# First MLP product of a hybrid encoder layer: Strassen's seven half-size products, with blocks of x1 kept in SBUF and in DRAM

## The chip, the cores and the metric

The kernel runs on one core of a Trainium2 chip. The metric is the device time of one execution in microseconds (us), lower is better.

## What is computed

The reference is one layer of a streaming encoder for 1024 tokens of width 1024 in float32: a LayerNorm, a mixer (stick-breaking attention, a Conformer convolution and a short gated convolution, joined by an output projection), a second LayerNorm whose result is called x1 here, and an MLP with a residual and a last LayerNorm:

```python
h = layer_norm(DEEPNORM_ALPHA * h + mix, ln_mix_g[l], ln_mix_b[l])          # x1, 1024 x 1024
ff = jnp.square(jax.nn.relu(h @ w_ff1[l])) @ w_ff2[l]                       # 1024 -> 4096 -> 1024
h = layer_norm(DEEPNORM_ALPHA * h + ff, ln_ff_g[l], ln_ff_b[l])
```

Only the MLP and the way into it bear on this change.

## The kernel before

Every large product is done in float32r, with each operand split in two: `split` (L126) has ScalarE cast the source to a high part h (L127) and VectorE subtract h from the source to get a low part l (L128). A product is then the three matmuls h·h, h·l and l·h, added up in PSUM.

The mixer ends with eight token tiles of 128 rows, handled in the order 6, 7, 4, 5, 0, 1, 2, 3 (`mix_tile`, `mix_tiles`, L726 to L757). Each tile gets its matmuls with `w_out` (L629), its sums (L733), its LayerNorm statistics on ScalarE and GpSimd (L737 to L748, L90 to L92) and its two rows of LayerNorm on VectorE (L121, L123); after that it is a tile of x1 in `acc`. `x1_columns` transposes a tile on TensorE (L169) and splits it into `x1h` and `x1l`, which hold all of x1 with the model width on the partitions.

The MLP runs over eight groups of 512 hidden units (`ff_group`, L904). A group has two products.

- The first one, x1 with the group's columns of `w_ff1`, is plain. `load_cols` loads 128 columns of the weights and splits them; `ff1_chunk` (L794) does 24 matmuls of 128x512 for half of the tokens into one PSUM bank (L800), then ScalarE takes the ReLU (L804) and VectorE squares it (L805). Four units of 128 columns and two halves of the tokens make 8 x 24 = 192 matmuls. The result lies in `ra[0]` and `ra[1]`.
- The second one, with the group's 512 rows of `w_ff2`, already goes by Strassen's scheme in Winograd's form. The hidden units and the tokens, and the units and the output columns, are cut in two halves each; seven products of half the size stand for eight. `a_part` and `b_part` split the operands of each into a ring of five buffers; GpSimd and VectorE form the sums and differences (`gsum`, L819; `early_sums`, L920). Each product is 4 x 6 = 24 matmuls into four banks (`product`, L847). The banks are added to one or more quarters of `acc` between the products (`add_to`, L857 to L861): four of the seven products go on accumulating in the same banks, so that each intermediate state can be read.

PSUM has four banks with the tag `g` for these products, three with `t` for transposes and one with `o`. An order of the instructions on each engine is made when the program is built, by a planner with its own estimates: it takes what the program lists first among what it thinks ready. Each engine and each DMA queue then works strictly in that order; SyncE (SP) issues nearly all loads.

For the first group, work starts before all of x1 is there: the chunks for the token half of tiles 4 to 7 go first (L979 to L995). In the last group `finish_rows` (L876) does the last LayerNorm, for tokens 0 to 511 with GpSimd's help and for the others on VectorE alone.

Of the kernel before, what the change touches and what calls it, by code (L numbers as in the profile page):

```python
# [15 lines left out]
P = 128  # L16
D = 1024
# [24 lines left out]
def hybrid_layer(ctx: ExitStack, tc, x, meta_tokens, ln_in_g, ln_in_b, w_in, w_conf_dw, b_conf_dw,  # L42
# [40 lines left out]
    yscr = dr.tile([4, P, S], F32, name="yscr")  # L83

# [674 lines left out]
    def x1_columns(i):  # L759
        transpose_split(acc[:, order[i], :], P, x1h, x1l, order[i] * P)  # L760

# [13 lines left out]
    x1h = x1p.tile([P, KT, S], F32R, name="x1h")  # L775
    x1l = x1p.tile([P, KT, S], F32R, name="x1l")
    done = 0
    for i in range(FIRST, 8):
        run(mix_tiles(i, i + 1))
        while done < i - 1 and done < 2 * (i - FIRST + 1):  # L780
            x1_columns(done)
            done += 1
    x = acc[:, order[7], :]
    ln_rows_dve(x, x, P, lnq[order[7]], *norm)
# [7 lines left out]
    ra = {}  # L792

    def ff1_chunk(j, w, c):  # L794

        pg = ps_g([P, 512])
        i = 0
        for k in range(KT):
            for a, b in ((0, x1h), (0, x1l), (1, x1h)):
                nc.tensor.matmul(pg, lhsT=w[a][:, k, :], rhs=b[:, k, c * 512:(c + 1) * 512],  # L800
                                 start=(i == 0), stop=(i == 3 * KT - 1))
                i += 1
        sq = cst.tile([P, 512], F32, tag="sq", bufs=1, name="sq")
        nc.scalar.activation(out=sq, in_=pg, func=AF.Relu)  # L804
        nc.vector.tensor_tensor(out=ra[j // 2][:, j % 2, HALF[c]], in0=sq, in1=sq, op=ALU.mult)  # L805

    def ff1_open(g, j):
        if j % 2 == 0:
            ra[j // 2] = wA.tile([P, 2, S], F32, tag="ff", bufs=2, name="relu2")
        u = 4 * g + (j + 2) % 4  # L810
        return halves(load_cols(w_ff1, u * P))

    def ff1(g, j):
        w = ff1_open(g, j)
        for c in range(2):
            ff1_chunk(j, w, c)
# [3 lines left out]

    def ring(name):
        return ffp.tile([P, 2, 2, 512], F32R, tag="ring", bufs=5, name=name)

    def a_part(src):
        hl = ring("a_hl")
        split(hl[:, 0], hl[:, 1], src)
        return hl

    def b_part(src):
        hl = ring("b_hl")  # L830
        split(hl[:, 0], hl[:, 1], src)
        return hl

    def w2_load(g):

        rb = [ffp.tile([P, 2, D], F32, tag=f"w2_{h}", bufs=1, name=f"w2_{h}") for h in range(2)]
        for h in (1, 0):
            r0 = (4 * g + 2 * (1 - h)) * P
            nc.sync.dma_start(out=rb[h], in_=w_ff2[r0:r0 + 2 * P, :].rearrange("(u p) c -> p u c", p=P))
        return rb  # L840
# [9 lines left out]

    def add_to(th, n, banks, first, sums=None, tts=range(4)):
        for tt in tts:
            t = 4 * th + tt
# [9 lines left out]
    def ln_ff_rows():  # L863

        rows, banks = [], []
        for tag, row in (("t1", ln_ff_g), ("s1", ln_ff_b)):
            r = ffp.tile([P, D], F32, tag=tag, bufs=1, name="ln_ff")
            bcast_row(r, row[0], nc.sync)
            rows.append(r)
        for i in range(4):  # L870
            bk = ps_t([P, 512]) if i < 3 else ps_o([P, 512])
            nc.scalar.activation(out=bk, in_=rows[i // 2][:, HALF[i % 2]], func=AF.Copy, scale=ROOT_D if i < 2 else 1.0)
            banks.append(bk)
        return rows[1], banks[:2], banks[2:]

    def finish_rows(t, sm, fb, gps, bps):  # L876
# [5 lines left out]
        junk = raw_tile("junk")  # L882
        nc.scalar.activation(out=junk, in_=a, func=AF.Square, bias=mean, accum_out=sm[:, 2:3])
        y = f32(big(name="y")[:, 0])
# [6 lines left out]
        if t < 4:  # L891
# [4 lines left out]
        for n in range(2):  # L896
            nc.vector.scalar_tensor_tensor(out=a[:, HALF[n]], in0=y[:, HALF[n]], scalar=rs[:, 0:1], in1=bps[n],
                                           op0=ALU.mult, op1=ALU.add)
            if t == NT - 1:
                (nc.sync, nc.scalar)[n].dma_start(out=os_[rows, HALF[n]], in_=a[:, HALF[n]])  # L900
        if t < NT - 1:
            nc.sync.dma_start(out=os_[rows, :], in_=a)

    def ff_group(g, opened=()):  # L904
# [5 lines left out]
        t1 = ffp.tile([P, 2, 512], F32, tag="t1", bufs=1, name="t1")  # L910
        gsum(t1, b12, b11, ALU.subtract)
        gsum(b12, b22, b12, ALU.subtract)
        for j in (2, 3, 0):
            if j not in opened:
                ff1(g, j)
        a11, a21 = (ra[0][:, :, h] for h in HALF)
        a12, a22 = (ra[1][:, :, h] for h in HALF)
        s1 = ffp.tile([P, 2, 512], F32, tag="s1", bufs=1, name="s1")

        def early_sums(u, eng):  # L920
            eng.tensor_tensor(out=s1[:, u], in0=a21[:, u], in1=a22[:, u], op=ALU.add)
            eng.tensor_tensor(out=a21[:, u], in0=a11[:, u], in1=a21[:, u], op=ALU.subtract)

        early_sums(0, nc.gpsimd)
        w = ff1_open(g, 1)
        ff1_chunk(1, w, 0)
        b, a = b_part(b21), a_part(a12)
        b_, a_ = b_part(b11), a_part(a11)
        gsum(b11, b22, t1, ALU.subtract)
        gsum(b21, b21, b11, ALU.subtract)  # L930
        gsum(a11[:, 0], s1[:, 0], a11[:, 0], ALU.subtract)
        ff1_chunk(1, w, 1)
        early_sums(1, nc.vector)
# [92 lines left out]
```

## Time and profile before

| | us |
|---|---|
| median of 3 runs | 1265.03 (1262.49 to 1266.19) |
| the profiled execution | 1265.27 |
| its span, first to last instruction | 1263.5 |

The profile is of one execution. It gives the busy time of each engine (PE is TensorE, PEld its weight loads, DVE VectorE, ACT ScalarE, POOL GpSimd, SP SyncE) and the chain of waits that ended last. A stretch's table tells what each engine did in that time, and the granted clock of TensorE as a share of 2.4 GHz. A matmul's own duration includes its way through the pipeline, so that its price in a dense row is the time from start to start.

### The profile page before, as it was taken

What the parts mean: (1) busy time and instruction counts of PE and PEld (TensorE: products, weight loads), DVE (VectorE), ACT (ScalarE), POOL (GpSimd) and SP (SyncE); (2) the same over time, 40 slices, a digit from 0 to 9 for tenths busy, and PEclk for the clock granted to TensorE, in tenths of its full rate; (3) what the DMA queues carried; (4) which work ended last, traced back from release to release, by engine and by line L of the source; (5) the groups of instructions that cost most, each with busy time, mean ns of one, the idle gap of its engine ahead of it and who ended that gap; (6) DMA issues with size and microseconds to landing.
All of it is one profiled execution on the core that took longest, in us unless ns stands there. A gap on an engine that the chain in (4) does not pass through costs nothing.

```text
span 1263.5 us, 15743 instructions
## 1 busy us (share of the span) xinstructions
PE 1186.0 (94%) x6126; PEld 1023.2 (81%) x6126; DVE 923.3 (73%) x1236; ACT 478.9 (38%) x883; POOL 235.3 (19%) x275
## 2 busy tenths in 40 slices
PE   5999996899989798998999999999999999999993
PEld 5999996789888687886888888888888888888882
DVE  6799976978788699777494684846947559467388
ACT  5522115656566445444332222313323123232244
POOL 2300002010000100144221312213212131121215
PEclk9999997989999899998999999999999999999997
DMA  9313111021011611203121111111211212012013
GB/s 291 121 39 86 59 51 51 17 51 34 17 34 51 200 34 67 84 16 102 34 67 34 50 67 34 52 65 35 82 30 38 67 50 84 18 51 67 1 34 133
DMA packets 71466, 78.97 MB, mean 63 GB/s; under 512 B 2345, under 2 KB 57936, under 8 KB 71392
## 3 DMA queue, kind: packets, MB, share of 16 engines
q1 hardware_dynamic: 67168, 67.97, 17.1%
q0 software_dynamic: 2304, 4.20, 1.7%
q10 hardware_dynamic: 1920, 5.81, 1.3%
q8 instruction: 48, 0.79, 0.3%
q14 instruction: 26, 0.21, 0.1%
HBM read 63.28 MB, written 10.49 MB: 58 GB/s over the span
## 4 chain that ended last, share of the span: by engine, by line
PE 67%; DVE 9%; ACT 3%; issue 2%; POOL 1%; DMA 1%; DVEq 0%; ACTq 0%; SPq 0%
PE ps_g L800 28%; PE ps_g L847 22%; PE ps_g L209 6%; PE ps_g L629 5%; DVE keepp L462 2%; PE ps_t L512 2%; PE ps_g L454 2%; PE ps_o L485 1%; PE ps_o L488 1%; DVE beta L464 1%; ACT keepp L458 1%; DVE acc L861 1%; DVE al L128 1%; DMA q_hl<-q_hl 1%; DVE a_hl L128 1%
## 5 line engine op out<-in xcount | busy, mean ns | idle before, releaser
L847 PE MATMUL ps_g<-b_hl,a_hl 128*128 128x512 f32 x1344 | 306.2, 389 | 2.3 <-DVE a_hl L128 2.3
L800 PE MATMUL ps_g<-x1h,w_hl 128*128 128x512 f32 x992 | 307.3, 389 | 0.0
L847 PEld LDWEIGHTS ps_g<-b_hl,a_hl 128*128 128x128 f32 x1344 | 252.2, 188 | 55.1 <-DVE a_hl L128 2.7
L209 PE MATMUL ps_g<-xh,w_hl 128*128 128x346 f32 (+4 forms) x1024 | 260.8, 334 | 0.9 <-ACT beta L459 0.9
L800 PEld LDWEIGHTS ps_g<-x1h,w_hl 128*128 128x128 f32 x992 | 186.2, 188 | 38.5
L800 PE MATMUL ps_g<-x1l,w_hl 128*128 128x512 f32 x496 | 193.0, 389 | 0.0
L805 DVE TENSOR_TENSOR relu<-sq 128x512 f32<-128x512 f32 x64 | 56.2, 878 | 185.9 <-ACT sq L804 185.9
L209 PEld LDWEIGHTS ps_g<-xh,w_hl 128*128 128x128 f32 x1024 | 181.4, 193 | 10.0 <-ACT beta L459 1.1
L209 PE MATMUL ps_g<-xl,w_hl 128*128 128x346 f32 (+4 forms) x512 | 171.0, 334 | 0.7 <-DVE xl L128 0.7
L804 ACT ACTIVATE sq<-ps_g 128x512 f32<-128x512 f32 x64 | 38.3, 598 | 285.4 <-PE ps_g L800 284.7
L859 DVE TENSOR_TENSOR acc<-ps_g,acc 128x512 f32<-128x512 f32 x192 | 126.5, 681 | 14.5 <-PE ps_g L847 13.5
L800 PEld LDWEIGHTS ps_g<-x1l,w_hl 128*128 128x128 f32 x496 | 93.1, 188 | 19.4
L209 PEld LDWEIGHTS ps_g<-xl,w_hl 128*128 128x128 f32 x512 | 99.0, 193 | 5.0 <-DVE xl L128 1.0
L128 DVE TENSOR_TENSOR w_hl<-raw,w_hl 128x1024 fp32r<-128x1024 f32 x59 | 93.2, 1580 | 11.8 <-ACT w_hl L127 11.6
L127 ACT CAST a_hl<-relu 128x1024 fp32r<-128x1024 f32 x48 | 50.5, 1053 | 123.6 <-PE ps_g L847 78.2
L462 DVE TENSOR_TENSOR_SCAN keepp<-keepp 128x912 f32<-128x912 f32 (+7 forms) x64 | 87.7, 1380 | 11.4 <-ACT keepp L458 10.9
L128 DVE TENSOR_TENSOR a_hl<-relu,a_hl 128x1024 fp32r<-128x1024 f32 x48 | 70.6, 1470 | 24.1 <-ACT a_hl L127 23.8
L127 ACT CAST w_hl<-raw 128x1024 fp32r<-128x1024 f32 x59 | 61.8, 1047 | 61.5 <-PE ps_g L209 31.7
L284 DVE SCALAR_TENSOR_TENSOR cacc<-glu,prm,cacc 128x482 f32<-128x482 f32 (+3 forms) x120 | 82.7, 743 | 0.3
L128 DVE TENSOR_TENSOR b_hl<-w,b_hl 128x1024 fp32r<-128x1024 f32 x48 | 67.1, 1398 | 0.5 <-ACT b_hl L127 0.2
L629 PE MATMUL ps_g<-w_hl,y 128*128 128x512 f32 x240 | 65.2, 409 | 1.8 <-DVE w_hl L128 1.7
L454 PE MATMUL ps_g<-ks,q_hl 128*128 128x456 f32 (+8 forms) x224 | 58.6, 364 | 8.4 <-ACT beta L459 3.9
(194 smaller groups left out, 1556.1 us busy)
## 6 DMA issues: line engine op xcount, KB each, us to landing
raw<-in_w_ff_dram SPq DMA_DIRECT2D x32, 512.0 KB, 4.1
w<-in_w_ff_dram SPq DMA_DIRECT2D x16, 1024.0 KB, 5.0
raw<-in_w_in_dram SPq DMA_DIRECT2D x22, 512.0 KB, 4.2
xt<-in_x_dram SPq DMA_DIRECT2D x8, 512.0 KB, 5.8
h_scr<-ht ACTq DMA_DIRECT2D x8, 512.0 KB, 3.2
q_hl<-q_hl POOLq DMA_DIRECT2D x16, 256.0 KB, 3.1
raw<-in_w_out_dram SPq DMA_DIRECT2D x8, 512.0 KB, 3.6
acc<-h_scr SPq DMA_DIRECT2D x8, 512.0 KB, 7.3
```

The lines of the kernel that those rows point to most:

```text
L127: nc.scalar.copy(out=h, in_=src)
L128: nc.vector.tensor_tensor(out=l, in0=src, in1=f32(h), op=ALU.subtract)
L209: nc.tensor.matmul(dst[:, :cw], lhsT=w[:, a, k, :], rhs=b[:, k, c0:c0 + cw], start=(i == 0), stop=(i == 3 * KT - 1))
L284: nc.vector.scalar_tensor_tensor(out=acc, in0=glu[j][:, o + k:o + k + n], scalar=prm[:, j, k:k + 1], in1=acc, op0=ALU.mult, op1=ALU.add)
L454: nc.tensor.matmul(zp[:, :cm], lhsT=qs[h][:, m, i * P:(i + 1) * P], rhs=ks[:, h, c0:c0 + cm], start=(m == 0), stop=(m == 1 and not last))
L462: nc.vector.tensor_tensor_scan(out=rev, data0=rev, data1=rev, initial=1.0, op0=ALU.mult, op1=ALU.bypass)
L629: nc.tensor.matmul(dst, lhsT=y[a][:, t * P:(t + 1) * P], rhs=w[b][:, n * 512:(n + 1) * 512], start=(i == 0), stop=(i == last))
L800: nc.tensor.matmul(pg, lhsT=w[a][:, k, :], rhs=b[:, k, c * 512:(c + 1) * 512], start=(i == 0), stop=(i == 3 * KT - 1))
L804: nc.scalar.activation(out=sq, in_=pg, func=AF.Relu)
L805: nc.vector.tensor_tensor(out=ra[j // 2][:, j % 2, HALF[c]], in0=sq, in1=sq, op=ALU.mult)
L847: nc.tensor.matmul(banks[tt], lhsT=a[:, x, u, tt * P:(tt + 1) * P], rhs=b[:, y, u, :], start=(start and i == 0), stop=(i == 5), skip_group ...
L859: nc.vector.tensor_tensor(out=a, in0=banks[tt], in1=a, op=ALU.add)
```

## The change

The first product goes by the same seven products. The group's 1024 x 512 weights are cut in halves both ways (a11, a12, a21, a22, each 512 x 256), x1 in halves of tokens and of width. Of x1's seven blocks and block combinations, each split in high and low, three stay in SBUF (`xt1`, `xt2`, `xt3`); the others share two tiles, X and Y, and come from the DRAM tensor `xscr` in each group, 2 MB each. Only the first group finds the first two in place. `x1_first` transposes and splits the plain blocks of the last four token tiles; `x1_second` forms differences of the token halves on GpSimd, and transposes and splits them and another plain block, of which two go to DRAM by way of `stage`.

A product is two banks of 12 matmuls (`product1`). Between products the banks are copied by ScalarE (`keep_sum`) or added to such a copy, and squared after a ReLU, by VectorE (`relu2`, `relu2_bank`). The weights of a group are loaded in two DMAs of 1 MB; GpSimd forms the weight sums s1, a21, a11 and a12 in place. In the second product the order of the seven products is another, the sums of the hidden values go to VectorE (`vsum`), the ring has four buffers in place of five, and which half of the tokens counts as the first is swapped (`tok`).

The core of the diff (loads, names and the last LayerNorm's buffers left out; what is not shown of the second product is its unchanged chain):

```diff
+    xscr = dr.tile([4, P, 2, 4, 512], F32, name="xscr")
...
-    def x1_columns(i):
-        transpose_split(acc[:, order[i], :], P, x1h, x1l, order[i] * P)
...
+    xb21, xb11, xt1, xt3 = [x_tile(x1p, tag) for tag in ("X", "Y", "T1", "T3")]
+
+    def x1_block(hl, src, cols):
+        pt = ps_t([P, 4, P])
+        for k in range(4):
+            nc.tensor.transpose(out=pt[:, k], in_=src[:, k * P:(k + 1) * P], identity=ident)
+        split(hl[:, 0, :, cols], hl[:, 1, :, cols], pt)
...
+    for i, x in enumerate((xb21, xb11)):
+        nc.sync.dma_start(out=xscr[i], in_=f32(x))
...
+    def product1(a, x, banks, start):
+        for j in range(2):
+            i = 0
+            for k in range(4):
+                for u, v in ((0, 0), (0, 1), (1, 0)):
+                    nc.tensor.matmul(banks[j], lhsT=a[:, u, k, j * P:(j + 1) * P], rhs=x[:, v, k, :],
+                                     start=(start and i == 0), stop=(i == 11), skip_group_check=True)
+                    i += 1
...
+    def keep_sum(r, th, bk):
+        for j in range(2):
+            nc.scalar.copy(out=r[:, j, HALF[th]], in_=bk[j])
+
+    def relu2(r, th, bk):
+        for j in range(2):
+            a = r[:, j, HALF[th]]
+            nc.vector.tensor_tensor(out=a, in0=bk[j], in1=a, op=ALU.add)
+            nc.vector.scalar_tensor_tensor(out=a, in0=a, scalar=0.0, in1=a, op0=ALU.max, op1=ALU.mult)
...
+    def x1_second(i, dt, stage):
+        t = order[i]
+        cols = slice(t * P, (t + 1) * P)
+        x, y = acc[:, t], acc[:, 4 + t]
+        d1, d2, d3, d4 = (dt[:, n // 2, HALF[n % 2]] for n in range(4))
+        gsum(d1, x[:, HALF[0]], y[:, HALF[0]], ALU.subtract)
+        gsum(d2, x[:, HALF[1]], d1, ALU.subtract)
+        gsum(d3, x[:, HALF[1]], x[:, HALF[0]], ALU.subtract)
+        gsum(d4, y[:, HALF[1]], d2, ALU.subtract)
+        x1_block(xt2, d2, cols)
+        x1_block(xt1, d1, cols)
+        c = slice(t % 2 * P, t % 2 * P + P)
+        x1_block(stage[0], x[:, HALF[1]], c)
+        x1_block(xt3, d3, cols)
+        x1_block(stage[1], d4, c)
+
+    def first_product(g, start=None):
...
+        s1 = raw_tile("s1").rearrange("p (k c) -> p k c", k=4)
+        gsum(s1, a21, a22, ALU.add)
+        gsum(a21, a11, a21, ALU.subtract)
...
+        if first:
+            pc, aa = start
+        else:
+            x = load_x("X", 0)
+            a = part(a12, 4)
+            pc = banks(2)
+            product1(a, x, pc, True)
+            aa = part(a11, 4)
+        keep_sum(r0, 0, pc)
+        x = xb11 if first else load_x("Y", 1)
+        pa = banks(2)
+        product1(aa, x, pa, True)
+        relu2(r0, 0, pa)
+        gsum(a11, s1, a11, ALU.subtract)
+        a = part(a11, 4)
+        if first:
+            second_half()
+        product1(a, xt2, pa, False)
+        keep_sum(r1, 0, pa)
+        gsum(a12, a12, a11, ALU.subtract)
+        a = part(s1, 4)
+        product1(a, xt1, pa, False)
+        keep_sum(r1, 1, pa)
+        x = load_x("X", 2)
+        a = part(a12, 4)
+        product1(a, x, pa, False)
+        relu2_bank(r0, 1, pa)
+        a = part(a21, 4)
+        pb = banks(2)
+        product1(a, xt3, pb, True)
+        relu2(r1, 1, pb)
+        x = load_x("Y", 3)
+        a = part(a22, 4)
+        product1(a, x, pb, False)
+        relu2(r1, 0, pb)
+        return r0, r1
...
+        b, a = part(b11, 2), part(a11, 2)
+        gsum(b11, b12, b11, ALU.subtract)
+        vsum(s1, a21, a22, ALU.add)
+        vsum(a21, a11, a21, ALU.subtract)
+        vsum(a11, s1, a11, ALU.subtract)
+        pa = banks(4)
+        product(a, b, pa, True)
+        add_to(0, 0, pa, first)
...
+    def second_half():
+        for n in range(2):
+            stage = [ring("stage").rearrange("p s (k c) -> p s k c", k=4) for _ in range(2)]
+            for i in (4 + 2 * n, 5 + 2 * n):
+                x1_second(i, ffp.tile([P, 2, D], F32, tag=f"w2_{i % 2}", bufs=1, name="diffs"), stage)
+            for j in range(2):
+                nc.sync.dma_start(out=xscr[2 + j][:, :, :, 256 * n:256 * n + 256], in_=f32(stage[j]))
```

## Rows read from the trace of the kernel before

**Rows 1.** The page's first part: busy us, share of the span, instructions.

```profile
PE 1186.0 (94%) x6126; PEld 1023.2 (81%) x6126; DVE 923.3 (73%) x1236; ACT 478.9 (38%) x883; POOL 235.3 (19%) x275
```

**Rows 2.** Stretches: length, busy us of each engine, granted clock, DMA share, GB/s.

```profile
601.38:634.35 32.97, 32.97 (x145) 27.29 (x146) 14.62 (x15) 10.25 (x13) 8.34 (x5) 1.00 0.12 32
...
754.03:797.55 43.52, 43.52 (x194) 36.04 (x193) 18.04 (x15) 10.99 (x14) 10.16 (x5) 1.00 0.13 37
797.55:835.63 38.08, 38.08 (x170) 31.53 (x169) 34.43 (x42) 11.66 (x12) 7.77 (x4) 1.00 0.21 69
...
1205.55:1263.50 57.95, 38.38 (x169) 31.11 (x167) 50.45 (x89) 25.40 (x34) 19.04 (x22) 0.88 0.24 91
```

**Rows 3.** The chain of waits in order of time, one group: start, us, engine, line.

```profile
754.03 43.52 PE ps_g L800 x192
797.55 38.08 PE ps_g L847 x168
```

**Rows 4.** VectorE in order of time, a second product: start us, us, instruction.

```profile
800.16 1.22 DVE L128 TENSOR_TENSOR w_hl<-raw,w_hl 128x1024 fp32r<-128x1024 f32 x1
801.29 0.68 DVE L859 TENSOR_TENSOR acc<-ps_g,acc 128x512 f32<-128x512 f32 x1
801.89 0.68 DVE L922 TENSOR_TENSOR relu<-relu 128x512 f32<-128x512 f32 x1
802.49 0.68 DVE L859 TENSOR_TENSOR acc<-ps_g,acc 128x512 f32<-128x512 f32 x1
...
816.82 1.21 DVE L128 TENSOR_TENSOR b_hl<-w,b_hl 128x1024 fp32r<-128x1024 f32 x1
```

**Rows 5.** VectorE in order of time, where GpSimd works beside it.

```profile
778.14 3.41 DVE L128 TENSOR_TENSOR w_hl<-raw,w_hl 128x1024 fp32r<-128x1024 f32 x1
...
805.00 2.42 DVE L128 TENSOR_TENSOR a_hl<-relu,a_hl 128x1024 fp32r<-128x1024 f32 x1
...
823.31 1.28 DVE L859 TENSOR_TENSOR acc<-ps_g,acc 128x512 f32<-128x512 f32 x2
```

**Rows 6.** GpSimd in order of time, the same group and one sum of the last.

```profile
777.75 2.73 POOL L819 TENSOR_TENSOR w<-w,w 128x1024 f32<-128x1024 f32 x1
...
795.96 2.14 POOL L819 TENSOR_TENSOR relu<-s,relu 128x512 f32<-128x512 f32 x1 [4.33 <-DVE a_hl L128]
803.92 2.42 POOL L819 TENSOR_TENSOR relu<-relu,relu 128x1024 f32<-128x1024 f32 x1 [5.82 <-DVE relu L934]
823.27 2.41 POOL L819 TENSOR_TENSOR t<-w 128x1024 f32<-128x1024 f32 x1 [16.93 <-DMA w<-in_w_ff_dram]
...
1196.11 1.29 POOL L921 TENSOR_TENSOR s<-relu,relu 128x512 f32<-128x512 f32 x1 [7.64 <-DVE relu L805]
```

**Rows 7.** ScalarE in order of time, the first casts of two operand pairs.

```profile
813.99 1.05 ACT L127 CAST a_hl<-relu 128x1024 fp32r<-128x1024 f32 x1 [3.51 <-PE ps_g L847]
...
819.35 1.05 ACT L127 CAST a_hl<-relu 128x1024 fp32r<-128x1024 f32 x1 [3.36 <-PE ps_g L847]
```

**Rows 8.** DMA issues: transfer, queue, count, KB each, median us to landing.

```profile
w<-in_w_ff_dram SPq DMA_DIRECT2D x16, 1024.0 KB, 5.0
```

**Rows 9.** Stretches of 5 us on the way into the MLP, columns as above.

```profile
580.00:585.00 5.00, 3.17 (x13) 2.57 (x14) 5.00 (x7) 2.77 (x7) 1.70 (x5) 0.50 0.50 127
585.00:590.00 5.00, 5.00 (x20) 4.21 (x20) 3.93 (x6) 1.68 (x3) 0.00 (x0) 0.70 1.06 384
```

**Rows 10.** TensorE in order of time on the way into the MLP.

```profile
574.09 0.40 PE L629 MATMUL ps_g<-wo,y_low 128*128 128x512 f32 x1
576.99 1.73 PE L169 MATMUL ps_t<-ident,acc 128*128 128x128 f32 x8 [2.50 <-DVE x1l L128]
...
584.71 0.80 PE L800 MATMUL ps_g<-x1h,w_slot 128*128 128x512 f32 x1
```

**Rows 11.** VectorE in order of time, the last token tile's second LayerNorm row.

```profile
585.77 1.27 DVE L123 SCALAR_TENSOR_TENSOR acc<-acc,rs,norm 128x1024 f32<-128x1024 f32 x1
```

**Rows 12.** SyncE's queue in order of time: the first weights of the MLP.

```profile
565.44 17.21 SPq L139 DMA_DIRECT2D raw<-in_w_ff_dram  x3
```

More of the change, by code (lines that the diff above doesn't have):

```diff
@@ L779, in hybrid_layer @@
         run(mix_tiles(i, i + 1))
-        while done < i - 1 and done < 2 * (i - FIRST + 1):
-            x1_columns(done)
+        while done < 4 and done < 2 * (i - FIRST + 1):
+            x1_first(done)
             done += 1
@@ L784, in hybrid_layer @@
     ln_rows_dve(x, x, P, lnq[order[7]], *norm)
-    NG = NF // 4
-    HALF = slice(0, 512), slice(512, 1024)
[L792 to L816, printed above, removed]
+    for i, x in enumerate((xb21, xb11)):
+        nc.sync.dma_start(out=xscr[i], in_=f32(x))
+    attw.release()
+    x1q = pool("x1q", side="right")
+    xt2 = x_tile(x1q, "T2")
@@ new lines, in w1_block, with w1_load @@
+    def w1_block(k, c0):
+        raw = raw_tile("w1_raw").rearrange("p (k c) -> p k c", k=4)
+        nc.sync.dma_start(out=raw, in_=w_ff1[512 * k:512 * k + 512, c0:c0 + 256].rearrange("(k p) c -> p k c", p=P))
+        return raw
+    def w1_load(g):
+        rk = []
+        for k in (1, 0):
+            raw = wA.tile([P, 4, 512], F32, tag="w", bufs=2, name="w1_raw")
+            nc.sync.dma_start(out=raw, in_=w_ff1[512 * k:512 * k + 512, 512 * g:512 * g + 512].rearrange("(k p) c -> p k c", p=P))
+            rk.append(raw)
+        return rk[1], rk[0]
@@ L818, in gsum, with w1_view, vsum, part @@
+    def w1_view(hl):
+        return hl.rearrange("p s (k c) -> p s k c", k=4)
     def gsum(dst, a, b, op):
         nc.gpsimd.tensor_tensor(out=dst, in0=a, in1=b, op=op)
+    def vsum(dst, a, b, op):
+        nc.vector.tensor_tensor(out=dst, in0=a, in1=b, op=op)
     def ring(name):
-        return ffp.tile([P, 2, 2, 512], F32R, tag="ring", bufs=5, name=name)
-    def a_part(src):
-        hl = ring("a_hl")
+        return ffp.tile([P, 2, D], F32R, tag="ring", bufs=4, name=name)
+    def part(src, k):
+        hl = ring("hl").rearrange("p s (k c) -> p s k c", k=k)
@@ L863, in ln_ff_rows @@
     def ln_ff_rows():
-        rows, banks = [], []
-        for tag, row in (("t1", ln_ff_g), ("s1", ln_ff_b)):
-            r = ffp.tile([P, D], F32, tag=tag, bufs=1, name="ln_ff")
+        rows, bks = [], []
+        for row in (ln_ff_g, ln_ff_b):
+            r = raw_tile("ln_ff")
             bcast_row(r, row[0], nc.sync)
@@ L909, in ff_group @@
         b21, b22 = (rb[1][:, :, h] for h in HALF)
-        t1 = ffp.tile([P, 2, 512], F32, tag="t1", bufs=1, name="t1")
+        t1 = raw_tile("t1").rearrange("p (u c) -> p u c", u=2)
         gsum(t1, b12, b11, ALU.subtract)
[L912 to L918, printed above, removed]
@@ L932, in ff_group @@
-        ff1_chunk(1, w, 1)
-        early_sums(1, nc.vector)
-        nc.vector.tensor_tensor(out=a11[:, 1], in0=s1[:, 1], in1=a11[:, 1], op=ALU.subtract)
-        def banks():
-            return [ps_g([P, 512]) for _ in range(4)]
-        pc = banks()
-        product(a, b, pc, True)
-        add_to(0, 0, pc, first)
-        pa = banks()
-        product(a_, b_, pa, True)
-        add_to(0, 0, pa, False, sums)
-        b, a = b_part(b11), a_part(a11)
-        gsum(a12, a12, a11, ALU.subtract)
+        gsum(b12, b22, t1, ALU.subtract)
@@ L958, in ff_group @@
-        pb = banks()
+        b, a = part(b21, 2), part(a12, 2)
+        gsum(b21, b21, b12, ALU.subtract)
+        pc = banks(4)
+        product(a, b, pc, True)
+        add_to(0, 0, pc, False, sums)
+        b, a = part(b11, 2), part(a21, 2)
+        pb = banks(4)
         if not last:
@@ L965, in ff_group @@
             return
-        b_, a_ = b_part(b21), a_part(a22)
-        for t in range(4):
-            finish_rows(t, sums[t], *ln)
+        b_, a_ = part(b21, 2), part(a22, 2)
+        for tt in range(4):
+            finish_rows(tok(0, tt), sums[tok(0, tt)], *ln, True, False)
         for step in (0, 1, 4, 2, 5, 3, 6, 7):
             tt = step % 4
+            t = tok(1, tt)
             if step < 4:
```

123 lines of the change are left out of this document (67 added, 56 removed).

## The prediction

> **What bounds the kernel now.** I read the busy times first: TensorE 1186.0 us of a span of 1263.5, VectorE 923.3 [rows 1]. A share over the whole span says little, so the next view is the table of stretches, for the stage that the change touches [rows 2]. From 601.38 us to 1205.55 us TensorE is busy in every microsecond of every stretch, at full clock. A group of the MLP takes 81.60 us: 43.52 for the first product and 38.08 for the second. The chain of waits says the same in its own way: for a whole group it names nothing but matmuls, x192 in 43.52 us, then x168 in 38.08 us [rows 3]. Both give 0.2267 us for a matmul of 128x512 (43.52/192 and 38.08/168), so here time is the number of matmuls. VectorE is the next engine: 18.04 us of the first stretch, but 34.43 us of the 38.08 of the second [rows 2]. That second number is where I expect the trouble.
>
> **What the change removes.** A unit of the first product takes 2x24 matmuls, a group of four 192. Seven products of 24 are 168, which is what the second product already has. So each group loses 24 x 0.2267 = 5.44 us of matmuls; eight groups lose 43.5 us. If TensorE stayed as dense, a group would take 76.16 us.
>
> **What it adds to VectorE and GpSimd in groups 1 to 7.** Durations from start to start: a split's subtraction of 1024 columns 1.13 us, an addition of a PSUM bank 0.60, a half-size sum 0.60 [rows 4]. The evictions of the first product become six pairs of bank addition and multiplication (0.6 each, the latter taken as a half sum) and two multiplications alone, in place of eight: 8.4 for 4.8. Splits go from 18 to 21 (+3.4). Sums on VectorE go from three of 512 to four of 1024 (+2.7). So some 53 us undisturbed, where the same count gives 44 before (measured 18.04+34.43 = 52.47 [rows 2]; the rest is time in which GpSimd held it up). GpSimd has eight sums of about 2.4 us, 19 us, near its 10.16+7.77 = 17.93 before. ScalarE has three more casts (1.05) and two instructions of 0.6 in place of two: +3 on 10.99+11.66 = 22.65 us, far from a bound.
>
> The disturbance is visible: a split of 1.13 us took 3.41 us at 778.14, beside a sum of GpSimd from 777.75 to 780.48, and 2.42 us at 805.00 beside one from 803.92; the two bank additions at 823.31, beside GpSimd's sum from 823.27, took 1.28 together, as ever [rows 5, 6]. A split that meets a sum loses some 1.3 us (2.42-1.13), up to 2.3; below I take 1.25.
>
> Now the second product's 38.08 us of matmuls. Before: 11 splits (12.4), 28 additions (16.8), three half sums and one multiplication (2.4) make 31.6, and 2.8 of holding up gives the measured 34.43. After: 13 splits (14.7), 28 additions (16.8), two full sums (2.3) and the tail of the last eviction (1.2) make 35. GpSimd's sums in this stretch go from three to four or five (the next group's weights are now summed here): at 1.25 each 5 to 6 us. Together 40 to 41 us, which is 2 to 3 us over. The overrun may run on into the next first product, where VectorE has some 24 of 38 us to do (8 splits 9.0, evictions 7.2, two sums 2.3, held up 5). TensorE feels it only when an operand pair is late. A pair's casts start when the product two before it lets go of its buffers, and take two casts and two splits: from 813.99 on ScalarE to 818.0 on VectorE (816.82+1.21); the next pair's casts, released by TensorE in the same way, began at 819.35, so 1.3 us were spare [rows 4, 7]. The ring of five buffers becomes one of four, which leaves that pattern. I put half of the overrun on TensorE, 1.2 us a group; the bounds are 0 and 3.
>
> **Bank handovers in the first product.** Before, a bank was reused three chunks later, 16 us. Now four products add onto banks that an engine must read between two products: 2.72 us (12 x 0.2267) from the end of a bank's product to its next use. ScalarE's copy (some 0.6, twice) fits; VectorE's addition (some 0.7, twice) fits unless it finds VectorE in a held-up split. Included in the 1.2 above; priced alone as a rival.
>
> **Reloads.** Four blocks of 2 MB a group come back: 8 MB on top of the 4 MB of weights. 12 MB in 76 us is 158 GB/s; 1 MB landed in 5.0 us, and a stretch moved 384 GB/s at a full DMA share [rows 8, 9]. Block X is asked for a second time when its first product is over, and needed three products later, 16.3 us; 2 MB take 6 to 10 us. Behind it on SyncE's queue wait block Y (four products of slack) and the group's w2 (five), which need 6 MB in some 33 us, 182 GB/s. Covered, so nothing; without the cover a late block would cost its lateness, up to 4 us.
>
> **Group 0 and the way in.** The last matmul of the mix starts at 574.09, and the last token tile's LN ends at 587.0 (585.77+1.27) [rows 10, 11]. Before, 48 matmuls were done between transposes by 601.38 and the other 144 ran to 634.35 [rows 2]. After, products one and two need only the first four tiles (48 matmuls, done by about 594). Product three needs the differences of all tiles: 14 of 16 GpSimd sums of 512 columns at 1.29 (2.14 if VectorE holds them up, [rows 6]), and three sums of weights at 2.4, 25 to 37 us from about 580, then a transpose and split, 2 us: 607 to 619, I take 610. Its 80 transposes, at 1.73 for eight at the low clock [rows 10], are 17 us at most, and its 20 bank splits 12 on VectorE: both lie beside GpSimd's chain. TensorE idles some 10 us; the granted clock stood at 0.50, the 1.2 GHz level, after waits like the 2.5 us before 576.99, and a matmul took 0.80 us instead of 0.40 [rows 9, 10]: +2. The other 120 matmuls take 27.2: 639, which is 5 later than 634.35. The rebuilt X block must be written (1 MB, 5 us) and read back (2 MB, 6 to 10) while two products (10.9) run: 0 to 4 more, I take 1. So group 0 loses 6 us; bounds -5 (all hidden) and +16. On SyncE's queue the two writes of 2 MB of the first blocks are new; 4 MB at 384 GB/s are 10.9 us. The early weights stand behind them in the program. In the kernel before, the early weights were asked for at 565.44, ahead of any x1 block [rows 12], and the planner can do the same again: nothing, and up to 10 if it doesn't (within the +16).
>
> **The last group.** VectorE does 50.45 of the last 57.95 us [rows 2], so its extra splits and sums (2.8 us) reach the end in part: +2, bounds 0 and +5.
>
> **The sum.** Groups 1 to 7: 7 x (-5.44 + 1.2) = -29.7. Group 0 +6, the end +2: -21.7. The profiled execution took 1265.27 us (span 1263.5 and 1.8 around it); the median of the three runs is 1265.03, the same. 1265.3 - 21.7 = 1243.6 us.
>
> **The rivals.**
> 1. *Dense all through.* The overrun stays off TensorE (0.15 a group), the way in and the end cost 1 each: 7 x (-5.44+0.15) + 2 = -35, 1230. For it: 604 us without one gap [rows 2], though VectorE was at 90% in each second product. Against it: GpSimd's chain before product three.
> 2. *VectorE and GpSimd take turns.* If GpSimd's sums held VectorE up for their whole length, 53 + 19 = 72 us of 76, and in the second product 35 + 4.5 x 2.4 = 46 us, of which 4 or 5 can run over: each group about 79.6 us, 7 x (-2.0), and with +8 for head and end 1259. For it: the 3.41 us split [rows 5]. Against it: additions from PSUM ran beside GpSimd unharmed, and they are nearly half of the work there. The Trainium skill has this as a rule: in its page SBUF — State Buffer, section "Who interferes with whom", a VectorE instruction with two SBUF inputs and a GpSimd instruction that reads SBUF lock each other out for a whole instruction, while one with a single SBUF input goes free. The trace agrees in both halves (3.41 us for one split, 1.28 for two additions).
> 3. *Slower: the bank handovers.* Only two banks for a product, each read between two products. If a bank's end finds VectorE in a held-up split (3.41) with another queued (1.13), the addition ends 3.41+1.13+0.68 = 5.2 after it, 2.5 past the 2.72. There are two such handovers on VectorE and two on ScalarE; 2.5 twice and 0.5 twice are 6 us a group, more than the 5.44 gained. 7 x 0.6 and +8 give 1277. It turns to a loss from 1.4 us a handover. For it: a split of 3.41 us does occur in the first product [rows 5]. Against it: VectorE has 24 of 38 us to do there, so a second one in its way is rare.
> 4. *It doesn't do what it says*: a reload that lands late each group. It would need less than 2 MB in 16.3 us, 123 GB/s, against 200 and more; 5 us late each time gives 7 x (-0.4) + 8, 1270.
>
> **How the numbers follow.** Forecast 0.48, rival 1 0.20, rival 2 0.15, rival 3 0.14, rival 4 0.03. The forecast's own range is 1230 to 1258. Reaching down to the dense case and up past rival 2, towards a part of rival 3, 1223 to 1271 should hold 8 in 10. A measurement of this kernel tells 0.3% from no change, 3.8 us: faster is under 1261.5. Forecast (0.46), rival 1 (0.20) and half of rival 2 (0.08) are faster, 0.74; same 0.09 (the rest of rival 2, a tail of the forecast); slower 0.17 (rival 3, rival 4).
>
> **What the next profile should show.** Matmuls of the first product x1344 in place of x1536; groups 1 to 7 at 77 to 78 us in the chain; TensorE's short gaps, if any, ahead of the second product's middle and released by VectorE's splits; VectorE above 36 us in each second product; a gap of about 10 us on TensorE near 595 to 610 whose releaser is a transposed difference from GpSimd. I'd be wrong if group time is 81 or more (look for bank waits released by VectorE), if the first wait in a group is a DMA, or if product three starts after 620 or before 600.

## The result, and the profile after

| | us |
|---|---|
| kernel before, median of 4 runs | 1263.76 (1260.05 to 1266.19) |
| changed kernel, median of 4 runs | 1275.84 (1274.51 to 1277.15) |
| ratio, 95% interval | 1.0098 (1.0069 to 1.0127) |
| profiled execution after, and its span | 1276.05, 1273.9 |

The change makes the kernel slower by 1%; the forecast was 1243.6 us. The page's first part, to be laid beside [rows 1]:

```profile
PE 1172.6 (92%) x5982; PEld 992.1 (78%) x5982; DVE 1020.6 (80%) x1328; ACT 508.3 (40%) x919; POOL 294.9 (23%) x291
```

TensorE has less to do than before and the span is 10.4 us longer, so the loss is waiting. The chain of waits names where. Before, a whole group was two lines of matmuls [rows 3]. After, one group reads so (start us, us, engine, line; pieces shorter than about 1.1 us don't stand in this view):

```profile
854.26 32.03 PE ps_g L855 x140
898.10 1.20 DVE acc L909 x2
899.30 3.40 DVE hl L129 x3
902.71 1.14 DVE relu L839
904.95 1.29 DVE acc L909 x2
907.97 2.74 DVE hl L129
910.71 1.80 DVE acc L909 x3
914.24 2.96 DVE hl L129
917.24 5.34 PE ps_g L864 x22
923.74 1.23 DVE hl L129
925.57 3.06 DVE hl L129
928.66 5.28 PE ps_g L864 x22
934.14 32.03 PE ps_g L855 x140
```

The first product is still matmuls for 140 of its 168; from there on, and through the second, the chain is VectorE's for the most part. From 854.26 to 934.14 it is 79.88 us a group, not 81.60 as before and not 77.4 as forecast. The same group in the table of stretches, cut at the start plus 38.06 us (168 matmuls); then the way in, group 0 and the end (length; busy us of PE, PEld, DVE, ACT, POOL; granted clock, DMA share, GB/s; compare [rows 2]):

```profile
854.26:892.32 38.06, 38.06 (x168) 31.51 (x169) 21.08 (x24) 12.30 (x16) 7.59 (x3) 1.00 0.58 215
892.32:934.14 41.82, 40.21 (x171) 31.01 (x169) 41.73 (x45) 13.07 (x13) 15.07 (x5) 1.00 0.29 107
...
597.00:617.20 20.20, 12.33 (x72) 10.01 (x72) 11.91 (x18) 9.29 (x17) 19.06 (x15) 0.83 0.28 91
617.20:656.14 38.94, 34.17 (x144) 26.54 (x143) 22.93 (x25) 12.30 (x17) 7.40 (x3) 0.96 0.89 330
...
1212.00:1273.90 61.90, 43.07 (x170) 32.93 (x168) 56.21 (x94) 27.14 (x35) 19.67 (x21) 0.86 0.22 85
```

In the second product VectorE works 41.73 of 41.82 us, and TensorE's waits there end with its splits and additions: it is the engine that bounds. In the first it works 21.08 of 38.06.

The ledger, by the starts of the groups' first products in the chain (before: 634.35+38.08 = 672.43 for group 1, then 81.60 each; after: 694.33, then 774.41, 854.26, 934.14, and so on to 1173.98 for group 7):

| stretch | before | after | difference | forecast |
|---|---|---|---|---|
| all up to group 1 | 672.43 | 694.33 | +21.90 | +6 |
| groups 1 to 6 | 489.60 | 479.65 | -9.95 | -25.4 |
| group 7 and the end | 101.47 | 99.92 | -1.55 | -2.2 |
| span | 1263.5 | 1273.9 | +10.4 | -21.7 |

### The profile page after: what moved, and what is told of

Its sections match the earlier page's. It is cut to its first block, busy times and chain, and to the rows that moved or that the text cites. A ratio compares the mean times of both kernels' runs of the same rounds, so it can differ in the third digit from the quotient of the medians.

```text
span 1273.9 us, 15655 instructions
## 1 busy us (share of the span) xinstructions
PE 1172.6 (92%) x5982; PEld 992.1 (78%) x5982; DVE 1020.6 (80%) x1328; ACT 508.3 (40%) x919; POOL 294.9 (23%) x291
## 4 chain that ended last, share of the span: by engine, by line
PE 42%; DVE 28%; ACT 4%; DMA 3%; POOL 3%; issue 3%; DVEq 0%; SPq 0%; ACTq 0%; POOLq 0%
PE ps_g L855 18%; DVE hl L129 11%; PE ps_g L864 6%; PE ps_g L210 6%; PE ps_g L630 5%; DVE acc L909 4%; DVE keepp L463 2%; DVE relu L839 2%; PE ps_t L513 2%; DMA xscr<-stage 1%; PE ps_g L455 1%; PE ps_o L486 1%; POOL diffs L836 1%; PE ps_o L489 1%; DVE relu L880 1%
## 5 line engine op out<-in xcount | busy, mean ns | idle before, releaser
L864 PE MATMUL ps_g<-hl 128*128 128x512 f32 x1344 | 323.8, 396 | 15.3 <-DVE hl L129 12.0
L864 PEld LDWEIGHTS ps_g<-hl 128*128 128x128 f32 x1344 | 250.5, 189 | 86.2 <-DVE hl L129 25.4
L855 PE MATMUL ps_g<-x_T,hl 128*128 128x512 f32 x576 | 134.0, 390 | 0.5 <-ACT relu L873 0.5
L855 PEld LDWEIGHTS ps_g<-x_T,hl 128*128 128x128 f32 x576 | 107.8, 188 | 23.2 <-ACT relu L873 0.9
L129 DVE TENSOR_TENSOR hl<-w_raw,hl 128x1024 fp32r<-128x1024 f32 x47 | 83.6, 1778 | 48.6 <-ACT hl L128 48.5
L129 DVE TENSOR_TENSOR hl<-relu,hl 128x1024 fp32r<-128x1024 f32 x48 | 99.5, 2072 | 1.3 <-ACT hl L128 1.3
L855 PE MATMUL ps_g<-x_Y,hl 128*128 128x512 f32 x384 | 92.8, 395 | 5.2 <-DMA x_Y<-xscr 3.1
L855 PEld LDWEIGHTS ps_g<-x_Y,hl 128*128 128x128 f32 x384 | 73.1, 191 | 21.3 <-DMA x_Y<-xscr 3.5
L855 PE MATMUL ps_g<-x_X,hl 128*128 128x512 f32 x360 | 85.0, 391 | 1.5 <-issue 1.3
L855 PEld LDWEIGHTS ps_g<-x_X,hl 128*128 128x128 f32 x360 | 66.9, 188 | 18.3 <-issue 4.6
```

What stands on the lines that cost most here:

```text
L129: nc.vector.tensor_tensor(out=l, in0=src, in1=f32(h), op=ALU.subtract)
L855: nc.tensor.matmul(banks[j], lhsT=a[:, u, k, j * P:(j + 1) * P], rhs=x[:, v, k, :], start=(start and i == 0), stop=(i == 11), skip_group_c ...
L864: nc.tensor.matmul(banks[tt], lhsT=a[:, x, u, tt * P:(tt + 1) * P], rhs=b[:, y, u, :], start=(start and i == 0), stop=(i == 5), skip_group ...
```

## The experiments

Theory after the result: (a) in each group, GpSimd's sums hold VectorE's splits up for as long as they last, and in the second product TensorE pays for it; (b) in group 0, GpSimd's queue (weight sums, then differences) starts the third product late, and then the round trip of the rebuilt blocks through DRAM stands in the way. Rivals: VectorE's own new work is what is too much, the order in which the sums are made, and the reloads. But for the last two kernels, each time below is that of one execution, and the kernel before took 1263.5 to 1265.2 us on the same chips. Executions of one kernel differ by up to some 6 us, so the lengths of the groups in the traces carry the argument: within one run of the changed kernel they agree to 0.25 us. With each edit the planner orders the instructions anew, so that an edit can move more than the lines it names.

**The sums left out.** All eight `gsum` of a group's weights are gone and plain blocks stand where the sums were; splits, matmuls and evictions stay.

```diff
-        gsum(s1, a21, a22, ALU.add)
-        gsum(a21, a11, a21, ALU.subtract)
...
-        a = part(s1, 4)
+        a = part(a21, 4)
```

> The changed kernel without GpSimd's eight sums of weights in each group: plain blocks stand where the sums stood, so the MLP's result is another, and every cast, split, matmul and bank addition is kept. GpSimd then has nothing to do in groups 1 to 7. Theory lock: in the second product VectorE is late because five of GpSimd's sums hold up splits, some 7 us of its 41.7. Without them its 34.4 us fit under 38.08 and a group takes 76.2 to 76.6 us in place of 79.9; groups 1 to 7 give back 7 x 3.4 = 24 us, and a part of the wait ahead of the third product of group 0 goes too (the four sums there took 582.5 to 594.4). Rival, own work: VectorE's larger share of sums, additions and splits makes operand pairs late by itself; then a group stays at 79 to 80 us.

Measured: 1245.03 us, a group of 77.53, the third product of group 0 at 604.34 in place of 617.23. Its group in the table of stretches, cut as above:

```profile
756.72:794.78 38.06, 38.06 (x169) 31.53 (x168) 17.96 (x22) 12.50 (x16) 0.00 (x0) 1.00 0.59 217
794.78:834.24 39.46, 38.96 (x169) 31.30 (x168) 37.24 (x47) 13.08 (x13) 0.00 (x0) 1.00 0.30 111
```

Of the 3.74 us by which the second product runs over 38.08, 2.4 come with the sums; 1.4 stay without any, where the theory had 0.4 at most. These 1.4 arise where the second product begins. TensorE in order of time:

```profile
802.82 3.92 PE L864 MATMUL ps_g<-hl 128*128 128x512 f32 x16 [0.28 <-DVE hl L129]
806.92 27.48 PE L864 MATMUL ps_g<-hl 128*128 128x512 f32 x120 [0.18 <-DVE acc L909]
```

The 28 matmuls from 795.70 need 6.35 us at 0.2267 and the next start is 7.12 later; these 16 need 3.63 and take 4.10; the last 120 run without a wait. VectorE has no pause until 813.37 and several after, so here it is late over the first 13 us, with the last evictions, the sums of the hidden values and the first splits, and not over the stage as a whole. In group 0 GpSimd's sums cost 12.9 us of the third product's start, about what they take there (four from 582.52 to 594.43). But this kernel leaves work out; whether the sums cost by being done or by being on GpSimd, the next run tells.

**The sums on VectorE.** Nothing left out; all eight change the engine.

```diff
-        gsum(s1, a21, a22, ALU.add)
+        vsum(s1, a21, a22, ALU.add)
...
```

> The changed kernel with the eight sums of weights of each group on VectorE in place of GpSimd. Theory lock: a sum on GpSimd costs VectorE some 1.5 us of holding up where it falls into the second product, and 1.14 us of work if VectorE does it itself, so the move gains a little: the second product has 34.4 + 5 x 1.14 = 40.1 us of VectorE, and a group takes 78 to 78.5 us; if the order puts a part of the sums into the first product, where VectorE has 17 us free, 76.5 to 78. Rival, own work: nine more microseconds on the engine that is late make a group 82 us or more, and the run some 1290.

Measured: 1259.27 us, a group of 78.49, third product at 611.81. The stretches:

```profile
844.59:882.65 38.06, 38.06 (x169) 31.53 (x168) 23.02 (x27) 12.51 (x16) 0.00 (x0) 1.00 0.58 215
882.65:923.09 40.44, 39.64 (x170) 31.09 (x169) 40.44 (x50) 13.06 (x13) 0.00 (x0) 1.00 0.31 110
```

VectorE, which already had no time to spare in the second product, does eight more instructions a group and the group gets 1.4 us shorter. So doing the sums costs it less than having GpSimd do them beside it. VectorE in order of time in the changed kernel, with GpSimd's sums below, shows why:

```profile
907.87 2.83 DVE L129 TENSOR_TENSOR hl<-relu,hl 128x1024 fp32r<-128x1024 f32 x1
910.63 1.87 DVE L909 TENSOR_TENSOR acc<-ps_g,acc 128x512 f32<-128x512 f32 x3
912.42 1.21 DVE L129 TENSOR_TENSOR hl<-w,hl 128x1024 fp32r<-128x1024 f32 x1
913.55 0.68 DVE L909 TENSOR_TENSOR acc<-ps_g,acc 128x512 f32<-128x512 f32 x1
914.16 3.03 DVE L129 TENSOR_TENSOR hl<-relu,hl 128x1024 fp32r<-128x1024 f32 x1
...
925.48 3.13 DVE L129 TENSOR_TENSOR hl<-relu,hl 128x1024 fp32r<-128x1024 f32 x1
...
930.33 3.11 DVE L129 TENSOR_TENSOR hl<-w_raw,hl 128x1024 fp32r<-128x1024 f32 x1
```

```profile
901.65 4.46 POOL L836 TENSOR_TENSOR s<-w_raw 128x1024 f32<-128x1024 f32 x1 [17.39 <-DVE hl L129]
906.19 3.43 POOL L836 TENSOR_TENSOR w_raw<-w_raw 128x1024 f32<-128x1024 f32 x1
913.71 2.40 POOL L836 TENSOR_TENSOR w<-w,w 128x1024 f32<-128x1024 f32 x1 [4.09 <-DVE hl L129]
925.13 2.39 POOL L836 TENSOR_TENSOR t<-w 128x1024 f32<-128x1024 f32 x1 [9.02 <-DMA w<-in_w_ff_dram]
929.96 2.39 POOL L836 TENSOR_TENSOR w<-w,t 128x1024 f32<-128x1024 f32 x1 [2.44 <-DVE acc L909]
```

Each long split ends 1.1 us after the sum beside it: 910.70 after 909.62, 917.19 after 916.11, 928.61 after 927.52, 933.44 after 932.35. That is its own undisturbed length (1.13 us from start to start), so it did nothing until the sum was over. The four lost (2.83+3.03+3.13+3.11) - 4 x 1.22 = 7.2 us. The first sum had it the other way round: a split and a sum of VectorE were ahead of it until 903.75, and it took 4.46 us in place of 2.4. This is the lock that the Trainium skill describes in its page SBUF — State Buffer, section "Who interferes with whom": two SBUF inputs on VectorE against a GpSimd instruction that reads SBUF, for the whole instruction; the four ends agree with it to 0.1 us.

**The order of two sums.** In the second product a11' is formed first, and a21' from it; all weight sums stay on GpSimd.

```diff
-        vsum(a21, a11, a21, ALU.subtract)
         vsum(a11, s1, a11, ALU.subtract)
+        vsum(a21, a22, a11, ALU.subtract)
```

> The changed kernel, all sums on GpSimd, with one edit in the second product: a11' = s1 - a11 first, then a21' = a22 - a11', so that the operand that is wanted first waits for one sum less. Lock theory (sheer time of VectorE, 41.7 of 41.8 us): order alone changes nothing, a steady group stays at 79.7 to 80.1 us, 1274 to 1276. Chain theory (the operand's way through the sums sets the end): 0.6 us a group, as the same edit gave in both products together with the sums on VectorE (78.49 to 77.88): 79.3, 1270 to 1272.

Measured: 1269.14 us (before, median 1264.96); groups of 77.9 to 79.0, 78.7 on the mean. Both expectations were too high. The same edit in the kernel without sums gave nothing:

> The changed kernel without GpSimd's eight sums, as in the run before (77.5 us a group), and with one sum of the hidden values on VectorE moved behind another: a11 = s1 - a11 first, then a21 = a22 - a11, the same value. The second and third product of the second half of a group wait for a11, not for a21. Theory chain of sums: the 1.4 us that are left over 76.16 come from the chain of sums between the last eviction of the first product and the operands of the second product's second and third part; taking 1.14 us out of it leaves 76.2 to 76.7 us a group. Rival, sheer amount: VectorE is simply too full in the second product, and a group stays at 77.3 to 77.6 us.

Measured there: 1244.84 us and 77.52 a group, beside 1245.03 and 77.53. So the order does not act through the chain of the operand itself, which is there in both; it needs the sums on GpSimd. What it changes is how many splits meet one. The splits of over 2 us in two second products of the reordered kernel, VectorE in order of time: two in the group that took 77.9 us (773.50 to 851.41), three in the next, which took 78.75:

```profile
832.16 3.04 DVE L129 TENSOR_TENSOR hl<-relu,hl 128x1024 fp32r<-128x1024 f32 x1
848.84 2.81 DVE L129 TENSOR_TENSOR hl<-w_raw,hl 128x1024 fp32r<-128x1024 f32 x1
...
910.10 3.04 DVE L129 TENSOR_TENSOR hl<-relu,hl 128x1024 fp32r<-128x1024 f32 x1
921.40 3.22 DVE L129 TENSOR_TENSOR hl<-relu,hl 128x1024 fp32r<-128x1024 f32 x1
926.34 3.12 DVE L129 TENSOR_TENSOR hl<-w_raw,hl 128x1024 fp32r<-128x1024 f32 x1
```

The changed kernel has four in each of its groups 1 to 6, and 79.9 us. Four, three, two: about one microsecond of the group for each. The price isn't the same all the way down: without any sum, and so without a collision, the same order takes 77.52, only 0.4 less than with two. That the order itself brings the collisions down, and not some shift along with it, is read from these counts and not shown apart. But the count sets the length without the order too: in the kernel with the blocks in place, below, which has the old order, one group has three such splits, and it takes 79.14 us beside 79.8 to 80.0 of the others.

**The reloads.** Groups 1 to 7 use what lies in X and Y and load nothing; their products are then made with the wrong blocks.

```diff
-        x = x_tile(x1p, tag)
-        nc.sync.dma_start(out=f32(x), in_=xscr[i])
-        return x
+        if i > 1:
+            x = x_tile(x1p, tag)
+            nc.sync.dma_start(out=f32(x), in_=xscr[i])
+            held[tag] = x
+        return held[tag]
...
-        x = load_x("X", 2)
+        x = load_x("X", 2) if first else held["X"]
...
```

> The changed kernel without the reloads of groups 1 to 7: the blocks that lie in tiles X and Y after group 0 are used again, so the MLP's result is another; 56 MB less come from DRAM. Theory of the prediction: the reloads are covered and cost nothing, so a group stays at 79.9 us. Rival: the reloads take time from the group, by lateness or by taking the place of the weights' loads; then a group is shorter by more than 0.5 us.

Measured: 1274.49 us, groups of about 80 (772.29 to 852.27), no better than with the 56 MB. The reloads of groups 1 to 7 cost nothing.

**Group 0: the differences on VectorE.** The four `gsum` of `x1_second` become `vsum`.

> The changed kernel with the 16 differences of x1 in group 0 on VectorE (0.6 us each) in place of GpSimd, which did them from 594.4 to 617.2. Theory chain: the third product waited for that chain. On VectorE the differences can be done by 602 to 606, and the third product starts at 604 to 608 in place of 617.2; the first group ends 8 to 13 us earlier than 694.3. Rival, weights: the third product waits for the sums of weights or for the last tile's LayerNorm; then its start moves by less than 4 us. Rival, DRAM: the way of the rebuilt blocks through DRAM takes the place of the wait; then the third product starts early, but the group ends only 0 to 4 us earlier.

Measured: 1274.55 us, third product at 617.61. Nothing was gained. For one thing, the weight sums left on GpSimd held VectorE up where the differences now were (in order of time):

```profile
583.58 3.42 DVE L124 SCALAR_TENSOR_TENSOR acc<-acc,rs,norm 128x1024 f32<-128x1024 f32 x1 [1.25 <-POOL rs L93]
586.91 6.82 DVE L839 TENSOR_TENSOR diffs<-acc 128x512 f32<-128x512 f32 x4
```

The first four differences took 6.82 us; undisturbed a half-size sum is 0.60 [rows 4]. For another, TensorE waited 6.33 us for these differences, until 594.48, before it came to the last 20 matmuls of the second product, which began at 596.92 in place of 592.22. After 604 VectorE went without a pause through differences, bank splits and evictions: the queue had changed its engine, not its length.

**Group 0: the rebuilt blocks in place.** They are split straight into the tiles X and Y, which are free by then; the copy to DRAM is only for the later groups.

```diff
-        x1_block(stage[0], x[:, HALF[1]], c)
+        x1_block(stage[0], x[:, HALF[1]], cols)
...
-        x = load_x("X", 2)
+        x = built[0] if first else load_x("X", 2)
```

> The changed kernel with the two rebuilt blocks of group 0 written straight into tiles X and Y, and copied to DRAM from there for the later groups, in place of going to DRAM by way of the staging buffers and back. Theory DRAM: the waits of 1.2 and 3.1 us ahead of the seventh product and the two products at half clock (1.9 us) come from that way; the first group ends 5 to 8 us earlier than 694.3, with the third product still at 617. Rival: the blocks come back before they are needed in any case, or the later groups' first load waits for the new copies; then the first group ends within 2 us of 694.3, or the second group starts late.

Measured: 1269.95 us. From the start of the third product to the end of the first MLP product it is 29.6 us (619.88 to 649.43), against 38.9 in the changed kernel (617.23 to 656.14): 9.4 less. Group 1 starts at 690.17, only 4.2 earlier: the third product was 2.7 later, and the second MLP product of group 0 took 40.7 in place of 38.2. That is because TensorE had not idled all through the round trip: between 642.67 and 645.73 it did 12 matmuls of the second product there, 2.7 us that now come later. So the round trip cost about 6.7 us net (9.4 - 2.7), and the second product's overrun was in group 0 too: 156 matmuls left, 35.4 us, in 38.2.

**Together.** The eight sums on VectorE and the blocks in place:

> Both corrections that helped, together: the eight sums of weights on VectorE, and the rebuilt blocks of group 0 in place. If they are independent: groups of 78.5 us, the first group's end some 5 us ahead of 687.6, and 1254 us in all. If they collide (VectorE has sums, transposed blocks and evictions to do at the same time in group 0), the first group ends at 686 to 688 and the run is 1258.

Measured: 1257.25 us, groups of 78.49. In group 0 the gains don't add up: group 1 starts at 686.08, where it was 687.77 with the sums on VectorE alone, and the third product, at 611.81 there, is back at 617.02. With the new order of the sums in both products besides (a11' = s1 - a11, then a21' = a22 - a11'):

> The same two corrections and the sums in the other order, in both products: a11 ahead of a21, so that the third product of group 0 waits for two sums of weights in place of three, and the second product's second part for one sum less. Theory chain of sums: groups of 77.3 to 77.8 us and the first group's end 1 to 2 us earlier than without the order, 1246 to 1249 us in all. Rival, sheer amount: groups stay at 78.4 us and the run at 1253.

Measured: 1252.19 us, groups of 77.88. Here the order helped with no sum on GpSimd: VectorE has one instruction fewer in the second product's stretch (x49 and 39.62 us below, x50 and 40.44 in the kernel before this one): the first product's a21' is now formed later. This kernel was then timed against the one before, with another beside it that leaves some sums on GpSimd:

> The changed kernel with all eight weight sums on VectorE, the rebuilt x1 blocks written straight into the X and Y tiles in group 0, and a11' formed ahead of a21' in both products. In one look it took 1252.2 us beside 1263.5 of the kernel before, with a steady group of 77.88 us (before 81.60). Theory (VectorE held up by GpSimd is what the change lost in every group): 1250 to 1254 us, about 1% faster than before in every round. If the one look was chance: within 0.3% of before, 1260 to 1266.

> As c5_timed, but only five of the eight sums are on VectorE: the two that open the first product's weights, the next sum that falls in the second product, and the two of w2 that are made ahead. Three sums stay on GpSimd, in the first product, where VectorE has 12 us to spare in a row. Lock theory: what a GpSimd sum costs depends on where it falls. If the three stay in the first product they cost nothing, VectorE is 3.4 us a group lighter, and the group goes to 77.4 to 77.9 us, 1249 to 1252. If VectorE's own work in the second product is all that counts, no difference from c5_timed, 1252 +-1. If they slip into the second product, each costs 1.5 to 1.9 us of VectorE there: group 78.5 to 80, 1257 to 1268.

Measured: 1251.39 us, median of 4 runs, before 1264.96; ratio 0.9882 (0.9864 to 0.9900). The second: 1253.15, ratio 0.9907 (0.9893 to 0.9922). As built, four sums and not three stayed on GpSimd in the second, a21' among them. Both have groups of 77.88. Their stretches, all sums on VectorE first, then four on GpSimd:

```profile
762.16:800.22 38.06, 38.06 (x169) 31.54 (x168) 23.64 (x28) 12.41 (x16) 0.00 (x0) 1.00 0.59 217
800.22:840.04 39.82, 38.91 (x170) 31.30 (x168) 39.62 (x49) 13.07 (x13) 0.00 (x0) 1.00 0.31 110
```

```profile
762.48:800.54 38.06, 38.06 (x169) 31.54 (x168) 22.14 (x24) 12.52 (x16) 10.94 (x4) 1.00 0.59 217
800.54:840.36 39.82, 38.92 (x169) 31.30 (x168) 39.60 (x49) 13.07 (x13) 0.00 (x0) 1.00 0.31 110
```

The four sums fell in the first product, where one split took 3.41 us and another 1.97, and the group did not notice. Nor did the kernel before with two held-up splits in each second product, where VectorE was busy for 34.43 of 38.08 us. So in these kernels a lock cost the group something only where VectorE had no time to spare.

## Why the prediction was wrong, point by point

- *24 matmuls fewer a group*: right. A first product is 38.06 us without a gap, 5.46 less than 43.52 [rows 3].
- *Bank handovers (third rival)*: they cost nothing that the trace shows; TensorE is busy all through 854.26 to 892.32. Wrong rival, rightly kept small.
- *VectorE's work in the second product, 40 to 41 us*: nearly right, 41.73. Its own part, 41.73 - 7.2 = 34.5, is the 35 of the sum; what it is held up for is 7.2 in place of 5 to 6. Of the five sums four held a split up, and the price of such a collision was 1.8 us, not 1.25: I took the shorter of the two in [rows 5]. Before the change a second product had two such splits, of 2.42 and 2.48 us; now four, of some 3.
- *Half of the overrun on TensorE, +1.2 a group, at most 3*: **the step that failed.** 41.82 - 38.08 = 3.74, all of the overrun and beyond the bound. I let VectorE carry it over into the next first product, where it has 17 us free. It can't: what is late is an operand pair or a bank of the second product itself, and TensorE stops there (the chain above). VectorE's idle time in the next product comes too late, and the kernel with four sums on GpSimd shows the reverse: VectorE has less to do in the first product there (22.14 us against 23.64), and the group is no shorter. In the ledger it is 25.4 - 9.95 = 15.5 us of the 32.1 us between forecast and result.
- *The rivals*: the second, VectorE and GpSimd in turns, came nearest for the groups. It said 79.6 us a group; 79.9 was measured. Its lock is in the trace, but that the number came out is in part luck: it had VectorE at 46 us in the second product, with 4 or 5 of the excess carried on into the next, and measured are 41.73 and nothing carried on. Its total of 1259 missed by group 0 for the most part. The first, dense all through, gives a group that not even the kernel without sums reaches (77.53 against 76.16).
- *Group 0, +6*: **the second step that failed**, +21.9, beyond the bound of +16. The third product starts at 617.23, inside 607 to 619 but 7.2 after the 610 that I took. GpSimd's queue was the cause, as named; from its first weight sum on, in order of time, with the three sums and the end of its work left out:

```profile
582.52 2.39 POOL L836 TENSOR_TENSOR s<-w_raw 128x1024 f32<-128x1024 f32 x1
...
594.39 6.83 POOL L836 TENSOR_TENSOR diffs<-acc 128x512 f32<-128x512 f32 x4
601.20 4.94 POOL L836 TENSOR_TENSOR diffs<-acc,diffs 128x512 f32<-128x512 f32 x4
```

  It began at 582.5 rather than 580, and did four weight sums, not three, before the first difference. Without any weight sum the third product started at 604.34. The larger miss is the round trip, for which I took 1 us. The chain from the third product on:

```profile
619.12 6.46 DMA xscr<-stage
626.04 12.51 DMA xscr<-stage
638.62 10.17 DMA x_Y<-xscr
648.83 7.33 PE ps_g L855 x24
```

  I priced X alone, one write and one read. Y is rebuilt last and goes the same way behind X: a write of 12.51 us, a read of 10.17. The first product ends at 656.14; by my sum it was 640.4. Of these 15.8 us, 7.2 are the late start and 8.6 the round trip; the kernel with the blocks in place, 9.4 us shorter here, agrees with that. A part of the 8.6 is the clock. TensorE had waited 3.10 us for that block; the granted clock, 1.00 until 648.83, was 0.58 from there to 651.00, and the product took 7.33 us in place of 5.44. The +2 for the clock stands in my sum at the start of the third product, where it was not spent: the granted clock was 1.00 from 617.23 to 623.00.
- *The third product's wait is a transposed difference from GpSimd*: right, though the longest gap is 5.43 us (before 602.50) and not 10. Of the other signs in the list, x1344 matmuls, VectorE above 36 us in each second product and short gaps released by its splits came out; groups of 77 to 78 us did not. None of the three signs of being wrong appeared (79.9 us a group, no wait for a DMA first, 617.23): they stood too far out to catch this loss.
- *Reloads free in the steady groups*: right, shown by leaving them out. *The early weights ahead of the block writes on SyncE's queue*: right, asked for at 571.71, the writes at 583.62.
- *The last group, +2*: the last second product and the end take 61.90 us in place of 57.95, +3.9, inside the bound of +5.
- *In sum*: -21.7 forecast, +10.4 measured. Of the 32.1 between, 15.5 are the overrun of groups 1 to 6, 15.9 group 0, 0.7 the end. The gain is real, and both holes can be mended in part: with the sums where VectorE does not meet them and the blocks in place, the same change gives 1251.39 us. Even there group 1 starts at 684.45, 12.0 us later than before the change, with the third product at 615.99, and a group is 77.88 us, not 76.16.

What stays open: the 1.4 us by which the second product runs over without any weight sum, and 1.7 in the best kernel. In both, most of it is lost in the first 12 or 13 us of the second product: in the best kernel TensorE waits for a split before 807.08 and for an addition before 812.38, and from there does 120 matmuls without a wait, although VectorE is busy for 39.62 of the 39.82 us. So what VectorE has to do where the products change is the likely bound, and the work further on is not; no run took work from that place. Open too is why the third product of group 0 starts no earlier than 616 in the best kernel, with no weight sum on GpSimd.

## What to carry to other kernels

An overrun of a helper engine inside a stage is not evened out by its idle time in the next one if the stage's operands are what is late: compare busy time with length stage by stage, and count the whole excess. Then look inside the stage as well: a helper with time to spare over the whole can still be late at its start. Before moving work to GpSimd, look at what VectorE does in that stretch: where VectorE is full, a sum that it does itself (1.2 us) is cheaper than one that holds a split of its own up (1.8 us). Data rebuilt on the chip should not go through DRAM to its first user; let the first user read it in place, and write the copy for later.

## What the runs showed of the hardware

- A split held up by a GpSimd sum ends 1.08 to 1.09 us after the sum does, in four cases of one group: it waits for the whole instruction, then runs at its own length. Four additions from PSUM at 903.75, beside the sum that ran from 901.65 to 906.11, took 2.49 us together, 0.62 each, as without it.
- 1 MB from SBUF to DRAM took 6.46 us from 619.12, and the next 12.51 from 626.04. Beside the second ran a 2 MB read (asked for at 625.65) and two of 1 MB (from 629.51 on); the stretch from 625.65 to 638.62 shows the DMA engines full:

```profile
625.65:638.62 12.97, 12.50 (x55) 9.74 (x54) 7.58 (x8) 5.60 (x8) 2.69 (x2) 1.00 1.01 362
```

  The Trainium skill's page DMA: Bandwidth & Descriptors, section "Specifications", gives about 358 GB/s as the HBM limit of a core. The 362 here lies close to it, but it was no bound for these kernels: the changed kernel moved 433 GB/s from 641.40 to 648.83, with two 2 MB reads under way, and the kernel before 384 in 5 us [rows 9].
